# A planner's constants and one yield: new estimates for the order of a fused transformer trunk

## The chip, the cores and the metric

The kernel runs on one core of a Trainium2 chip. The metric is the device time of one execution in microseconds (us); lower is better. An execution is timed without the profiler several times, and once with it.

## What is computed

The reference is a trunk of two layers on 256 tokens of width 1024, all in float32. Each layer is, cut to what matters:

```python
h = h + 0.5 * swiglu(rmsnorm(h, ffn1_norm), ffn1_w_gate, ffn1_w_up, ffn1_w_down)   # 1024 -> 2752 -> 1024
u = rmsnorm(h, mix_norm)
z = u @ w_in                       # mLSTM q, k, v, o, i, f; attention q, k, v; two merge gates
hm = sigmoid(m_o) * head_rmsnorm(mlstm_chunkwise(mq, mk, mv, ig, lf))
ha = swa_gqa_sinks(aq, ak, av, a_sinks)          # 16 query heads, window 128
h = h + (sigmoid(g_m) * (hm @ w_branch_m) + sigmoid(g_a) * (ha @ w_branch_a)) @ w_out
h = h + 0.5 * swiglu(rmsnorm(h, ffn2_norm), ffn2_w_gate, ffn2_w_up, ffn2_w_down)
h = h + sigmoid(rmsnorm(h, ple_norm) @ ple_gate_w) * (p_i @ ple_proj_w)
```

## The kernel before

**Precision.** Every float32 operand of a matmul is split into a high and a low half of the type fp32r, `hi = cast(x)` on ScalarE and `lo = x - hi` on VectorE. A product is three matmuls: `xh·wh`, `xh·wl`, `xl·wh` (`mm3`). In the profile the halves of the weights are the tiles `wh` and `wl`, those of the normed activations `uT`.

**Tiles.** The 256 tokens are two token tiles (t = 0, 1) of 128 rows; the residual stream is `h0`, `h1`. A weight is loaded in pieces of one megabyte (`raw`, two buffers), each of two parts of 128x1024 values; a part is split into a ring of eight `wh`, `wl` buffers. A part of 128x1024 covers two blocks of 128 input features for 512 outputs.

**Stages.** In each layer: FFN 1, the mixer, FFN 2, and the gate on the layer's end (`ple`). An FFN starts with 512 gate and 512 up features by token (`gu`), goes on by feature (`pg`, `pu`) and ends with the down projection (`dn`). The mixer starts with attention's projections (`kvq`) and ends with the output projection (`yo`). `ple` first multiplies the per-layer input (`pp`, 24 matmuls) and then the gate (`pg`, 1024 outputs in two halves n = 0, 1). The tile `pg` is thus both FFN and layer-end gate.

**From one stage to the next.** At the end of a stage the two token tiles are finished one after the other. `sink` adds a half-row of 512 to `h` (VectorE), squares it with a sum (`sq`, ScalarE), and after the second half starts the next norm: `ms` (VectorE), a power of -1/2 on GpSimd (`r`), two scaled halves `xn` (VectorE), eight transposes `tp` on TensorE, and the split into `uT`. While that runs for token tile 0, TensorE has the rest of token tile 1: 22 matmuls after a `dn`, 24 after `yo`, 30 after the gate. For the gate, `use` puts ahead of the sum a tanh (ScalarE) and a product (VectorE), both on the tile `sg`.

**The order.** The four engines TensorE, ScalarE, VectorE and SyncE run their instructions in exactly the order in which the Python program writes them. What interleaves the stages is a planner that runs while the program is written. Side work is a generator (a chain); each `yield` marks a step. A class `Clock` keeps an estimated time for each engine: an instruction costs `fixed + n * per` (`COST`, for n values a row), a result counts for other engines `SYNC` later, and a load of a megabyte occupies the queue for `DMA[1]` and lands `DMA[0]` later. `now` is the estimated time of TensorE. Between groups of matmuls (every three of 512 columns in the stages named here) `tick` continues each chain whose last step is ready by that estimate, and then `feed` may begin the split of one more weight part, if its piece has landed by the estimate and ScalarE and VectorE are not too far ahead:

```python
    def tick(self):
        for chain in list(self.bg):
            if chain[1] <= self.clock.now:
                self.advance(chain)
        self.feed()
```

So the estimates change no instruction, but they decide where each one stands in its engine's order. `haste`, set near the end of token tile 0, holds further splits back once three parts are in store, until token tile 0's transposes are written. When a matmul needs a chain that isn't finished, `finish` moves the estimated clock forward until it is.

**The opening.** Row sets of `x` and the first pieces are loaded in the order: token tile 0 in two halves, first gate piece in two halves, token tile 1, second gate piece. The planner sets `ready` for the two norms from these loads.

## Time and profile before

| | |
|---|---|
| median of 3 runs | 1383.12 us (1381.99 to 1383.64) |
| profiled execution | 1383.27 us, span 1381.5 us, granted clock 0.998 |
| TensorE matmuls | 1366.2 us busy, 99% of the span, 9056 instructions |
| VectorE | 860.7 us, 62% |
| ScalarE | 734.8 us, 53% |
| GpSimd | 55.4 us, 4% |
| DMA | 243.81 MB, 176 GB/s on average |

In the rows of the profile that follow, the first number of a timeline row is the start in us from the begin of the span, the second the duration, then the engine, the operation, the tile written and those read, shapes, and in brackets the idle time of that engine before it and what ended it. PE is TensorE's matmuls, DVE is VectorE, ACT is ScalarE, POOL is GpSimd. Almost all rows carry the line L130, a helper that passes every instruction on, so the tile's name tells what a row is. In rows of busy time by stretch the columns are the stretch, its length, then busy time and count of PE, PEld, DVE, ACT and POOL, the granted clock of TensorE, the DMA share and GB/s.

### The profile page before, as it was taken

The numbers are of one execution on the slowest core, as the hardware profiler recorded it, in microseconds if no ns is written. First come the engines' busy times: TensorE is split into PE (matmuls) and PEld (weight loads), VectorE is DVE, ScalarE is ACT, GpSimd is POOL, SyncE is SP. The second block draws the span as 40 slices with busy tenths as digits, with TensorE's granted clock in tenths as the row PEclk, the third lists the DMA queues.
The fourth block names the chain that finished last, engine by engine and source line by source line (L and its number), as shares of the span: only waits on it lengthen the run. The fifth ranks groups of instructions, "written<-read, shape, count | busy, mean of one in ns | idle before, by whom it ended". The sixth has DMA issues, their size and how long they took to land.

```text
span 1381.5 us, 21941 instructions
## 1 busy us (share of the span) xinstructions
PE 1366.2 (99%) x9056; PEld 1233.3 (89%) x9056; DVE 860.7 (62%) x1213; ACT 734.8 (53%) x1146; POOL 55.4 (4%) x84
## 2 busy tenths in 40 slices
PE   8999999999999999999999999999999999999998
PEld 5999887899899899988879998878998998999886
DVE  5655458767786665554565554687677876554544
ACT  5554346878465444443454443477785554544433
POOL 0000012000000000000000000120000000000000
PEclk9999999999999999999999999999999999999999
DMA  6665636344645565565456566445456544755651
GB/s 206 222 212 168 229 125 212 123 138 110 226 153 185 167 213 186 169 232 184 158 162 213 170 199 213 152 154 173 106 143 206 181 156 164 220 190 187 209 180 61
DMA packets 125830, 243.81 MB, mean 176 GB/s; under 512 B 14977, under 2 KB 23841, under 8 KB 125730
## 3 DMA queue, kind: packets, MB, share of 16 engines
q1 hardware_dynamic: 125730, 242.41, 55.1%
q8 instruction: 71, 1.16, 0.4%
q14 instruction: 29, 0.24, 0.1%
HBM read 241.34 MB, written 1.05 MB: 175 GB/s over the span
## 4 chain that ended last, share of the span: by engine, by line
PE 96%; DMA 1%; DVE 1%; ACT 1%; issue 0%; POOL 0%; SPq 0%; ACTq 0%; POOLq 0%
PE dn L130 17%; PE pg L130 16%; PE pu L130 14%; PE gu L130 7%; PE z L130 7%; PE gt L130 7%; PE kvq L130 5%; PE ya L130 3%; PE v L130 3%; PE ym L130 3%; PE yo L130 3%; PE og L130 3%; PE tp L130 3%; PE sc L130 1%; PE ha L130 1%; DMA raw<-in_ffn_w_gate_dram 1%
## 5 line engine op out<-in xcount | busy, mean ns | idle before, releaser
L130 DVE TENSOR_TENSOR wl<-raw,wh 128x1024 fp32r<-128x1024 f32 (+1 forms) x448 | 540.2, 1222 | 351.3 <-ACT wh L130 348.5
L130 ACT CAST wh<-raw 128x1024 fp32r<-128x1024 f32 x448 | 460.5, 1050 | 414.1 <-PE dn L130 82.9
L130 PE MATMUL dn<-wh,hid 128*128 128x512 f32 x688 | 218.1, 395 | 0.0
L130 PE MATMUL pg<-uT,wh 128*128 128x256 f32 x1088 | 194.0, 281 | 0.0
L130 PE MATMUL pu<-uT,wh 128*128 128x256 f32 x1088 | 192.9, 280 | 0.0
L130 PEld LDWEIGHTS pg<-uT,wh 128*128 128x128 f32 x1088 | 166.4, 188 | 0.2
L130 PEld LDWEIGHTS pu<-uT,wh 128*128 128x128 f32 x1088 | 166.2, 188 | 0.0
L130 PEld LDWEIGHTS dn<-wh,hid 128*128 128x128 f32 x688 | 129.2, 188 | 30.2
L130 PE MATMUL pg<-uT,wl 128*128 128x256 f32 x544 | 152.4, 280 | 0.0
L130 PE MATMUL pu<-uT,wl 128*128 128x256 f32 x544 | 152.2, 280 | 0.0
L130 PE MATMUL dn<-wl,hid 128*128 128x512 f32 x352 | 139.0, 395 | 0.0
L130 PEld LDWEIGHTS pu<-uT,wl 128*128 128x128 f32 x544 | 102.4, 188 | 0.0
L130 PEld LDWEIGHTS pg<-uT,wl 128*128 128x128 f32 x544 | 102.3, 188 | 0.0
L130 PE MATMUL z<-uT,wh 128*128 128x256 f32 x512 | 93.5, 284 | 0.0
L130 PE MATMUL gt<-uT,wh 128*128 128x256 f32 x512 | 93.1, 283 | 0.0
L130 PE MATMUL gu<-wh,uT 128*128 128x512 f32 x256 | 83.4, 402 | 2.2 <-ACT uT L130 2.2
L130 PEld LDWEIGHTS gt<-uT,wh 128*128 128x128 f32 x512 | 78.8, 188 | 1.2
L130 PEld LDWEIGHTS dn<-wl,hid 128*128 128x128 f32 x352 | 66.1, 188 | 15.1
L130 PEld LDWEIGHTS z<-uT,wh 128*128 128x128 f32 x512 | 78.8, 188 | 0.6
L130 PE MATMUL z<-uT,wl 128*128 128x256 f32 x256 | 71.9, 281 | 0.0
L130 PE MATMUL gt<-uT,wl 128*128 128x256 f32 x256 | 71.8, 280 | 0.0
L130 PE MATMUL kvq<-wh,uT 128*128 128x512 f32 x192 | 63.7, 401 | 0.0
(194 smaller groups left out, 2037.7 us busy)
## 6 DMA issues: line engine op xcount, KB each, us to landing
raw<-in_w_in_dram SPq DMA_DIRECT2D x60, 1024.0 KB, 5.1
raw<-in_ffn_w_up_dram SPq DMA_DIRECT2D x40, 1024.0 KB, 5.1
raw<-in_ffn_w_down_dram SPq DMA_DIRECT2D x40, 1024.0 KB, 5.2
raw<-in_ffn_w_gate_dram SPq DMA_DIRECT2D x39, 1024.0 KB, 5.5
raw<-in_w_branch_a_dram SPq DMA_DIRECT2D x16, 512.0 KB, 5.9
raw<-in_w_branch_m_dram SPq DMA_DIRECT2D x8, 1024.0 KB, 5.1
raw<-in_w_out_dram SPq DMA_DIRECT2D x8, 1024.0 KB, 5.2
raw<-in_ple_gate_w_dram SPq DMA_DIRECT2D x8, 1024.0 KB, 8.0
```

Source lines behind the costliest of these rows:

```text
L130: return issue(*args, **kw)
```

## The change

The estimates get other values, an instruction with a sum along the row (`accum_out`) costs `SUM` more, and in `ple` the use of token tile 1's gate waits in the planner, in layer 0 alone, until token tile 0's `xn` of the next norm are written down. `normed` counts the norms of token tile 0 so far, four a layer.

```diff
-    COST = {"tensor": (0.0, 1 / 2400), "scalar": (0.12, 1 / 1120), "vector": (0.12, 1 / 960), "gpsimd": (0.3, 0.17)}
-    SYNC = 0.1
+    COST = {"tensor": (0.0, 1 / 2250), "scalar": (0.14, 1 / 1130), "vector": (0.16, 1 / 960), "gpsimd": (0.5, 0.17)}
+    SYNC = 0.2
+    SUM = 0.2
     TABLE = 1.4
-    DMA = (1.0, 2.9)
+    DMA = (2.0, 2.9)
...
-    def charge(self, engine, n, func=None):
+    def charge(self, engine, n, func=None, extra=0.0):
...
-        self.t[engine] = start + fixed + n * per
+        self.t[engine] = start + fixed + extra + n * per
...
                               args[2] if op == "activation" else None)
+                              self.clock.SUM if kw.get("accum_out") is not None else 0.0)
...
     def norm(self, t, ss, g, xT):
...
             nc.vector.scalar_tensor_tensor(xn[n], self.h[t][:, half(n)], r, g[n], op0=ALU.mult, op1=ALU.mult)
+        self.normed += t == 0
         yield
...
     def ple(self, l, xT, sink):
...
             def use(n, t, ps):
+                while t == NT - 1 and l < DEPTH - 1 and self.normed <= 4 * (l + 1):
+                    yield
                 sg = self.scr("sg")
                 nc.scalar.activation(sg, ps, AF.Tanh, scale=0.5)
```

## The prediction

> **What bounds the kernel now.** I read the totals of the page first, then the waits of TensorE, then the timeline engine by engine where those waits lie.

> ```profile
> span 1381.5 us, 21941 instructions
> PE 1366.2 (99%) x9056; PEld 1233.3 (89%) x9056; DVE 860.7 (62%) x1213; ACT 734.8 (53%) x1146; POOL 55.4 (4%) x84
> ```

> TensorE is busy for 1366.2 of 1381.5 us. No matmul is added or removed, so an order can only fill the 15.3 us that are left, or add to them. The waits of TensorE, in total, times and longest:

> ```profile
> PE tp L130 <- DVE xn L130: 3.9, 2, 3.0
> PE gu L130 <- ACT uT L130: 2.2, 1, 2.2
> PE sc L130 <- DVE ptd L130: 0.9, 2, 0.5
> PE gu L130 <- DVE wl L130: 0.8, 1, 0.8
> ```

> The 3.0 is the boundary between the layers. The 2.2, the 0.8 and 0.9 of the 3.9 lie in the opening, and the 0.9 in attention. Everything else follows without a gap.

> **The boundary between the layers.** Rows of TensorE, ScalarE, VectorE and GpSimd there:

> ```profile
> 690.55 0.40 PE L130 MATMUL pg<-wh,uT 128*128 128x512 f32 x1
> 693.93 1.88 PE L130 MATMUL tp<-ident,xn 128*128 128x128 f32 x8 [2.98 <-DVE xn L130]
> 697.86 0.40 PE L130 MATMUL gu<-wh,uT 128*128 128x512 f32 x1
> 698.09 0.39 PE L130 MATMUL gu<-wl,uT 128*128 128x512 f32 x1
> 702.41 0.50 PE L130 MATMUL gu<-wl,uT 128*128 128x512 f32 x1
> 686.88 1.05 ACT L130 CAST wh<-raw 128x1024 fp32r<-128x1024 f32 x1 [1.20 <-DMA raw<-in_ffn_w_gate_dram]
> 687.84 0.59 ACT L130 ACTIVATE sg<-pg 128x512 f32<-128x512 f32 x1
> 693.25 0.63 ACT L130 ACTIVATE sq<-h 128x512 f32<-128x512 f32 x1 [1.48 <-DVE h L130]
> 696.33 1.99 ACT L130 CAST wh<-raw 128x1024 fp32r<-128x1024 f32 x2
> 698.22 0.60 ACT L130 ACTIVATE sg<-pg 128x512 f32<-128x512 f32 x1
> 691.79 0.69 DVE L130 SCALAR_TENSOR_TENSOR sg<-sg,pp 128x512 f32<-128x512 f32 x1 [0.32 <-ACT sg L130]
> 693.13 1.41 DVE L130 SCALAR_TENSOR_TENSOR xn<-h,r,g 128x512 f32<-128x512 f32 x2
> 701.14 2.35 DVE L130 TENSOR_TENSOR wl<-raw,wh 128x1024 fp32r<-128x1024 f32 x2
> 691.55 0.55 POOL L130 TENSOR_TENSOR r<-ms,mhalf 128x1 f32<-128x1 f32 x1 [23.93 <-DVE ms L130]
> 693.90:697.80 3.90, 3.87 (x14) 3.41 (x15) 2.02 (x3) 2.61 (x5) 0.00 (x0) 0.56 0.02 4
> ```

> A matmul of 512 columns follows the last after 0.23 us (697.86 to 698.09). The 24 matmuls of token tile 1 ahead of 690.55 put the end of tile 0's gate at about 685.2. Its tanh runs only at 687.84, because a weight cast that waits for its DMA stands ahead on ScalarE. POOL has the norm's factor at 692.10, but xn starts at 693.13: the pair sg, h of tile 1's first half (691.79 to 693.2) stands ahead on VectorE. TensorE idles 2.98 us. Then the clock is at 0.56 of full speed (last row) until 697.8, and transposes and six matmuls take 3.93 us where 0.8 + 6 x 0.23 = 2.2 would do. The place costs about 3.0 + 1.7 = 4.7 us.

> **The change there.** The new condition makes tile 1's use (tanh, sg, h, square) wait in the planner until tile 0's xn are written down. VectorE then has xn at 692.14 in place of 693.13, 1.0 us sooner. How many matmuls the planner puts ahead of the transposes I work out by its own constants: tanh, two products, mean, power come to 2.77 us before and 3.41 after, which is 13.0 and 15.0 matmuls of its length (512/2400, 512/2250); it looks every 3 matmuls, so both resume at 15; xn end at 21.6 and 22.0, so both place the transposes after 24 of 30. The six matmuls stay behind them.

> Queued behind the moved work: on VectorE sg and h (2 x 0.7) now follow xn, which ends at 692.14 + 1.41 = 693.55, so h ends at 694.9; the square behind it on ScalarE needs 0.75, and the casts uT stand behind the square: they start at about 695.6, where they now start at 695.0. After them come two weight casts (1.99), tile 1's tanh, its two products, square and mean, and only then the wl at 701.14, which takes 2.92 us from that tanh. TensorE uses the first of these wl after 18 matmuls of gu: 697.86 + 4.2 = 702.03, and gets it at 702.41. So **the next thing that is late is wl**, and it does not come sooner: 696.33 becomes about 696.6, wl ends 0.2 to 0.3 later. TensorE starts gu a microsecond sooner and waits at the fourth gate part. Against that, a later DMA estimate (from 3.9 to 4.9 us for a megabyte) may move the weight cast's VectorE half behind the mean, 0.3 sooner. I take 0 for this place. Ends: +0.3 (as worked out), and -1.1 if the cast of 686.88 goes behind the tanh altogether: the chain then starts 2.3 us sooner, the square of tile 1 ends at 694.1, wl at 701.3.

> **The other boundaries.** Here the costs alone act, as the new condition holds at once. From FFN to mixer, rows of TensorE, ScalarE and VectorE:

> ```profile
> 197.49 1.03 PE L130 MATMUL tp<-ident,xn 128*128 128x128 f32 x8
> 198.28 0.48 PE L130 MATMUL dn<-wh,hid 128*128 128x512 f32 x1
> 198.59 0.39 PE L130 MATMUL dn<-wl,hid 128*128 128x512 f32 x1
> 198.85 0.48 PE L130 MATMUL kvq<-wh,uT 128*128 128x512 f32 x1
> 198.12 1.08 ACT L130 CAST uT<-tp 128x512 fp32r<-128x512 f32 x2
> 198.74 1.29 DVE L130 TENSOR_TENSOR uT<-tp,uT 128x512 fp32r<-128x512 f32 x2 [1.28 <-ACT uT L130]
> ```

> After tile 0's last sum there are 22 matmuls of tile 1. Old reckoning: h 0.75, square 0.68, mean 0.22, power 0.57 = 2.22 us, resumed at matmul 11 (2.35); xn 1.31 + 0.1 ends at 3.75 = 17.6 matmuls; next look at 20. The rows agree: two dn follow the transposes. New: h 0.89, square 0.79 + 0.2 (with its sum and the longer SYNC), mean 0.36, power 0.87 = 3.12 us = 13.7 matmuls, resumed at 14 (3.19); xn 1.39 + 0.2 ends at 4.77 = 20.97; next look at 22. So the two dn go ahead and nothing is left to cover uT. From the start of the transposes to the first uT takes 198.12 + 0.59 - 197.49 = 1.22 us, to the first low half 198.74 + 0.69 - 197.49 = 1.94. With transposes at 198.0 the third kvq matmul, which needs the low half, runs at 199.95 in place of 199.49; allowing for the matmul's own delay there, 0.38 us lost. It occurs in both layers: **+0.8**.

> From mixer to FFN:

> ```profile
> 477.38 1.03 PE L130 MATMUL tp<-ident,xn 128*128 128x128 f32 x8
> 478.17 0.47 PE L130 MATMUL yo<-wh,mT 128*128 128x512 f32 x1
> 478.94 0.40 PE L130 MATMUL gu<-wh,uT 128*128 128x512 f32 x1
> ```

> 24 matmuls are left, looked at every 3. Old: resumed at 12 (2.56), xn end at 3.97 = 18.6, placed at 21; three yo follow the transposes (478.17 to 478.94), as reckoned. New: resumed at 15 (3.41), xn end at 5.00 = 21.97, placed at 24, behind all yo. Transposes then start at 478.07, the low half is there at 480.0, where the third matmul of gu ran at 479.41: 0.56 us. Two layers: **+1.1**. From FFN to the gate of the layer's end the transposes slip as well, but 24 pp matmuls (5.6 us) lie ahead of the first use: 0.

> **The opening.** Rows of ScalarE, VectorE and TensorE:

> ```profile
> 8.29 1.04 ACT L130 CAST wh<-raw 128x1024 fp32r<-128x1024 f32 x1 [2.96 <-DMA raw<-in_ffn_w_gate_dram]
> 9.62 1.04 ACT L130 CAST wh<-raw 128x1024 fp32r<-128x1024 f32 x1 [0.29 <-DMA raw<-in_ffn_w_gate_dram]
> 10.57 1.07 ACT L130 CAST uT<-tp 128x512 fp32r<-128x512 f32 x2
> 11.53 0.64 ACT L130 ACTIVATE sq<-h 128x512 f32<-128x512 f32 x1
> 13.51 2.00 ACT L130 CAST wh<-raw 128x1024 fp32r<-128x1024 f32 x2 [0.64 <-DMA raw<-in_ffn_w_gate_dram]
> 14.34 1.41 DVE L130 SCALAR_TENSOR_TENSOR xn<-h,r,g 128x512 f32<-128x512 f32 x2 [0.67 <-POOL r L130]
> 15.67 1.22 DVE L130 TENSOR_TENSOR wl<-raw,wh 128x1024 fp32r<-128x1024 f32 x1
> 11.21 0.79 PE L130 MATMUL gu<-wh,uT 128*128 128x512 f32 x1 [2.24 <-ACT uT L130]
> 16.94 0.50 PE L130 MATMUL gu<-wl,uT 128*128 128x512 f32 x1 [0.80 <-DVE wl L130]
> ```

> Old reckoning: tile 0's xn are ready at 7.60, tile 1's rows at 8.50, so uT goes ahead of tile 1's squares: the rows show it (10.57, 11.53). New: tile 0's rows at 5.15, squares to 6.94, mean to 7.30, power to 8.17, xn to 9.75; tile 1's rows at 9.50. Its two squares (1.27 us: 10.57 + 1.07 against 12.8) are now put ahead of uT, and both wl of the first pieces ahead of uT's low half. The squares need tile 1's rows. These are half a megabyte, in the queue behind the piece that landed at 9.62 and ahead of the megabyte that landed at 13.51; an equal rate gives 9.62 + 3.89/3 = 10.9 (an estimate from these rows). So uT starts at 12.2, gu at 12.9 in place of 11.21: 1.7 later. Part comes back: wl at 15.67 now goes ahead of tile 1's xn and ends at 15.8, so the 0.80 is gone. But tile 1's transposes fall behind all 18 matmuls and uncover 0.4. The matmuls are slow at first, as a row of the busy times by stretch shows:

> ```profile
> 11.20:14.70 3.50, 3.50 (x8) 2.76 (x9) 2.83 (x5) 2.86 (x7) 0.55 (x1) 1.00 0.12 44
> ```

> Eight matmuls in 3.5 us are 0.44 each, nearly twice 0.23 (though the clock column says 1.00 there). With 3.5 us of that again from 12.9, the twenty-first matmul runs at 20.7 in place of 19.5: **+1.2**. Ends: +0.4 (rows landing by 9.6) and +2.0. The high end is a matter of when the slow stretch ends. If it ends on a grid of its own length, and not that long after the restart, the end after 14.7 is 18.2; from 12.9 the matmuls run at 0.44 until then, the twenty-first at 21.4, and the opening loses 1.9. [...]

> **Sum.** +1.2 + 0.8 + 1.1 + 0 = +3.1 us. The profiled execution took 1383.27 us, 0.15 over the median 1383.12; on the median this is 1386.2. Attention and recurrence change order too: their chains grow by about a tenth in matmuls, and TensorE's 0.9 us there can go or grow to 2: ends -0.9, +2.

> **Rivals.**
> - *The transposes stay.* The new places miss the old ones by one matmul in each case (20.97 against a look at 20, 21.97 against 21). If VectorE or ScalarE work is reckoned otherwise by that much, the 1.9 us vanish: 1384.3. Against it: the old reckoning met all four places exactly. Chance 0.17.
> - *Not slower: the boundary between the layers is cured.* If the DMA estimate moves the cast of 686.88 behind the tanh and wl ahead of tile 1's second half, all 4.7 come back: 1386.2 - 4.7 = 1381.5. It decides from 1 us: the cast's megabyte is issued early enough in the planner's time that I find its place 1.0 us ahead of the tanh under the new latency (2.4 before). Chance 0.17; with the opening unharmed as well it would pass below 1380.4.
> - *The busy window.* The slow stretch ends on its grid: the opening loses 1.9, 1386.9; and a recurrence chain late at ym adds up to 2: 1389. Chance 0.18.

> The forecast itself has 0.48 (own range 1385.3 to 1387.2). About 0.2% (2.8 us) is what a measurement of this kernel can tell from no change. Slower by more, above 1385.9: 0.30 of the 0.48 and most of the window's 0.18, together 0.46. Faster: half of the cure's 0.17 and a little, 0.10. Same: 0.44. The range, to leave no more than 2 in 10 out: 1381.5 to 1388.5.

> **What would show it.** Transposes of xn directly ahead of kvq and gu, with waits of TensorE on uT that aren't there now; squares ahead of uT in the opening and gu near 12.9; xn ahead of sg at the boundary between the layers, and gu waiting for wl at about 702 there. Wrong if the first gu comes before 11.5, if gu at that boundary runs through its fourth gate part before 701, or if the dn and yo rows after the transposes remain.

## The result and the profile after

The changed kernel takes 1402.37 us in the median (1401.27 to 1403.76, 4 runs) against 1382.55 us of the kernel before on the same chip: a ratio of 1.0151, 95% interval [1.0138, 1.0163]. It is slower by about 20 us, where 3 had been forecast. The profiled execution took 1403.76 us.

The totals of the changed kernel and its waits of TensorE (what was waited for, total us, times, longest; two waits ahead of the opening's `gu` and one of 0.5 on `mT` are left out):

```profile
span 1402.0 us, 21877 instructions
PE 1376.5 (98%) x9056; PEld 1238.5 (88%) x9056; DVE 858.0 (61%) x1213; ACT 734.9 (52%) x1148; POOL 52.6 (4%) x84
PE gu L132 <- ACT uT L132: 6.7, 5, 2.9
PE sc L132 <- ACT pr L132: 3.1, 3, 1.1
PE kvq L132 <- DVE wl L132: 1.8, 1, 1.8
PE kvq L132 <- ACT uT L132: 1.6, 2, 1.4
PE ym L132 <- DVE hmT L132: 1.1, 1, 1.1
PE ym L132 <- ACT hmT L132: 1.0, 1, 1.0
PE gu L132 <- DVE wl L132: 0.9, 2, 0.5
```

Two things grew. Waits stand where there were none (`sc` on `pr`, `kvq`, `ym`), and the busy time of the same 9056 matmuls is 10.3 us longer (1376.5 against 1366.2), half of the loss, which no wait accounts for. A halved clock, shown below, makes by estimate about 3.4 of it (three stretches of 1.7 us against one before) and a longer slow stretch in the opening about 1 (six more matmuls at 0.43 us in place of 0.23); the rest is spread over the stages and was not assigned. Both kernels run the same weight matmuls in the same sequence, so the start of the first matmul of a stage can be compared one to one:

| stretch | later by (us) | of which seen as |
|---|---|---|
| start to `dn`, layer 0 | +1.80 | first `gu` at 12.25 in place of 11.21, fourteen slow matmuls in place of eight |
| `dn`, `kvq` of layer 0 | +1.92 | wait of 1.36 on `uT` |
| attention and recurrence, layer 0 | -0.10 | a wait of 1.02 made good |
| `ym`, layer 0 | +5.90 | waits 0.99 and 1.13 on `hmT`, halved clock |
| `yo`, `gu`, layer 0 | +1.66 | wait of 1.20 on `uT` |
| FFN 2 | -0.17 | |
| gate of layer 0 to the features of layer 1 | -2.45 | the place that the condition is meant for |
| `dn`, `kvq`, layer 1 | +4.29 | wait of 1.78 on `wl`, halved clock |
| attention and recurrence, layer 1 | +2.55 | waits 1.06, 1.02 on `pr`, halved clock |
| `ym`, `yo`, `gu`, layer 1 | +4.56 | wait of 1.20 on `uT`, one on `mT` |
| the rest | +0.6 | |

The sum is +20.6. The boundary for which the prediction gave 0 is the only place that gained more than 0.2. The following rows are all of the changed kernel.

FFN to mixer, layer 0; timeline rows of TensorE, ScalarE and VectorE:

```profile
199.82 1.04 PE L132 MATMUL tp<-ident,xn 128*128 128x128 f32 x8
202.21 0.50 PE L132 MATMUL kvq<-wh,uT 128*128 128x512 f32 x1 [1.36 <-ACT uT L132]
200.97 0.63 ACT L132 ACTIVATE sq<-h 128x512 f32<-128x512 f32 x1 [2.12 <-DVE h L132]
201.60 1.05 ACT L132 CAST uT<-tp 128x512 fp32r<-128x512 f32 x2
200.25 0.68 DVE L132 SCALAR_TENSOR_TENSOR h<-dn,h 128x512 f32<-128x512 f32 x1
```

The transposes stand behind all `dn`, as forecast. But between them and their casts ScalarE has token tile 1's square, which waits for token tile 1's `h`, which needs the last `dn`. The cast starts at 201.60, 1.78 us after the first transpose, where the kernel before took 0.63 us (197.49 to 198.12): by that measure 1.1 us late.

The recurrence's end, `ym` of layer 0; the same engines:

```profile
453.68 0.38 PE L132 MATMUL ym<-hmT,wh 128*128 128x256 f32 x1 [0.99 <-ACT hmT L132]
455.19 0.54 PE L132 MATMUL ym<-hmT,wh 128*128 128x256 f32 x1 [1.13 <-DVE hmT L132]
451.36 2.00 ACT L132 CAST wh<-raw 128x1024 fp32r<-128x1024 f32 x2
453.25 0.38 ACT L132 CAST hmT<-tp 128x256 fp32r<-128x256 f32 x1
452.44 2.36 DVE L132 TENSOR_TENSOR wl<-raw,wh 128x1024 fp32r<-128x1024 f32 x2 [0.53 <-ACT wh L132]
454.72 0.42 DVE L132 TENSOR_TENSOR hmT<-tp,hmT 128x256 fp32r<-128x256 f32 x1
```

For token tile 1 both halves of the last head's `hmT` stand behind two weight casts each, 2.00 us on ScalarE and then 2.36 us on VectorE.

Mixer's start in layer 1, VectorE and TensorE:

```profile
898.11 1.03 PE L132 MATMUL tp<-ident,xn 128*128 128x128 f32 x8
901.85 0.51 PE L132 MATMUL kvq<-wl,uT 128*128 128x512 f32 x1 [1.78 <-DVE wl L132]
899.37 1.29 DVE L132 TENSOR_TENSOR uT<-tp,uT 128x512 fp32r<-128x512 f32 x2 [1.90 <-ACT uT L132]
900.57 3.49 DVE L132 TENSOR_TENSOR wl<-raw,wh 128x1024 fp32r<-128x1024 f32 x3
```

Three `wl` whose `wh` is long there stand behind token tile 1's `uT`. VectorE idles 1.90 us for that `uT`, and then TensorE idles 1.78 us for the first of the three.

The clock, in rows of busy time by stretch:

```profile
199.27:202.68 3.41, 2.05 (x14) 1.49 (x12) 1.71 (x6) 1.71 (x5) 0.55 (x1) 1.00 0.00 0
451.86:455.27 3.41, 1.28 (x10) 0.85 (x8) 2.75 (x4) 1.76 (x3) 0.00 (x0) 1.00 0.79 303
455.27:458.68 3.41, 3.41 (x16) 3.41 (x17) 0.00 (x0) 1.05 (x1) 0.00 (x0) 0.50 0.75 244
899.00:902.41 3.41, 1.63 (x8) 1.04 (x7) 3.04 (x4) 0.82 (x2) 0.00 (x0) 1.00 0.00 0
902.41:905.82 3.41, 3.41 (x9) 2.63 (x8) 2.25 (x5) 0.00 (x0) 1.01 (x1) 0.50 0.83 266
936.54:939.95 3.41, 1.55 (x7) 0.80 (x6) 1.98 (x5) 3.40 (x17) 3.41 (x2) 1.00 0.00 0
939.95:943.36 3.41, 3.19 (x16) 2.26 (x16) 1.86 (x7) 2.92 (x11) 0.41 (x9) 0.50 0.00 0
```

After the stretches with 2.13, 1.78 and 1.86 us without a matmul (3.41 less the PE column) the clock is at 0.50 for 3.41 us, which costs by estimate up to half of that, 1.7 us. After 1.36 us without a matmul (first row) it stays at 1.00, until 455.27. So the wait of 1.78 us at `kvq` cost by estimate up to 3.5 with what followed.

The opening (one row of it from the kernel before, line L130) and attention:

```profile
12.25 0.80 PE L132 MATMUL gu<-wh,uT 128*128 128x512 f32 x1 [2.88 <-ACT uT L132]
17.96 0.58 PE L132 MATMUL gu<-wl,uT 128*128 128x512 f32 x1
18.38 0.63 PE L132 MATMUL gu<-wh,uT 128*128 128x512 f32 x2
18.85 0.40 PE L132 MATMUL gu<-wl,uT 128*128 128x512 f32 x1
14.78 0.65 PE L130 MATMUL gu<-wh,uT 128*128 128x512 f32 x2
10.39 0.63 ACT L132 ACTIVATE sq<-h 128x512 f32<-128x512 f32 x1 [0.20 <-DMA h<-in_x_dram]
11.63 1.05 ACT L132 CAST uT<-tp 128x512 fp32r<-128x512 f32 x2
245.58 0.38 PE L132 MATMUL sc<-band,identb 128*128 128x512 bf16 x1 [1.02 <-ACT pr L132]
241.33 1.28 ACT L132 ACT_TABLE_LOAD   x1
```

In the opening both squares of token tile 1 are ahead of `uT`, as forecast; its rows landed by 10.39, half a microsecond sooner than estimated. The matmuls are slow for longer than before: fourteen of them, one every 0.43 us, from 12.25 until 18.38, where the spacing falls to 0.23 (two in 0.47 us). In the kernel before, eight were slow, from 11.21 until 14.78. In attention the next scores wait 1.02 us for eight exponentials (242.63 to 245.44) that stand behind the table load of 1.28 us.

The boundary between the layers:

```profile
696.33 0.60 ACT L132 ACTIVATE sg<-pg 128x512 f32<-128x512 f32 x1 [0.30 <-PE pg L132]
705.07 1.05 ACT L132 CAST uT<-tp 128x512 fp32r<-128x512 f32 x2
705.68 0.50 PE L132 MATMUL gu<-wh,uT 128*128 128x512 f32 x1 [1.19 <-ACT uT L132]
711.15 0.50 PE L132 MATMUL gu<-wl,uT 128*128 128x512 f32 x1 [0.51 <-DVE wl L132]
```

ScalarE idles 0.30 us until token tile 0's gate is done and then runs its tanh at once; no cast with a DMA wait stands ahead of it any more. But the transposes stand behind 27 of token tile 1's 30 matmuls and not 24, and `uT` is 1.19 us late behind a square of token tile 1. `wl` is late at the fourth gate part, as forecast, by 0.51.

### The profile page after: what moved, and what is told of

It is laid out like the page before. It is cut to its first block, busy times and chain, and to the rows that moved or that the text cites. A ratio compares the mean times of both kernels' runs of the same rounds, so it can differ in the third digit from the quotient of the medians.

```text
span 1402.0 us, 21877 instructions
## 1 busy us (share of the span) xinstructions
PE 1376.5 (98%) x9056; PEld 1238.5 (88%) x9056; DVE 858.0 (61%) x1213; ACT 734.9 (52%) x1148; POOL 52.6 (4%) x84
## 3 DMA queue, kind: packets, MB, share of 16 engines
HBM read 241.34 MB, written 1.05 MB: 173 GB/s over the span
## 4 chain that ended last, share of the span: by engine, by line
PE 93%; DVE 3%; ACT 2%; DMA 1%; issue 1%; SPq 0%; POOL 0%; ACTq 0%
PE dn L132 17%; PE pg L132 15%; PE pu L132 14%; PE gu L132 7%; PE z L132 7%; PE gt L132 7%; PE kvq L132 5%; PE ya L132 3%; PE og L132 3%; PE yo L132 3%; PE v L132 3%; PE ym L132 3%; PE tp L132 2%; PE sc L132 1%; PE ha L132 1%; DVE wl L132 1%
## 5 line engine op out<-in xcount | busy, mean ns | idle before, releaser
L132 PEld LDWEIGHTS gu<-wh,uT 128*128 128x128 f32 x256 | 49.1, 193 | 21.2 <-ACT uT L132 8.2
```

The lines of the kernel that those rows point to most:

```text
L132: return issue(*args, **kw)
```

## Experiments

**The condition alone.** All constants as before (and SUM 0); only this stays of the change:

```diff
+        self.normed += t == 0
...
+                while t == NT - 1 and l < DEPTH - 1 and self.normed <= 4 * (l + 1):
+                    yield
```

> The old constants with the new condition alone. Up to the boundary between the layers its order is that of before, so what it changes lies there. Theory Y (the 2.8 us that the changed kernel wins at that boundary come from the condition): 1379.5 to 1381.5. Rival C (they come from the constants, which move a weight cast behind the tanh; the condition alone only brings the next wait forward, as the prediction had it): 1382.3 to 1383.3.

1381.63 us, ratio 1.0001 [0.9992, 1.0010]. TensorE's waits at the boundary, from its timeline:

```profile
691.63 1.32 PE L132 MATMUL tp<-ident,xn 128*128 128x128 f32 x8 [1.30 <-DVE xn L132]
694.86 0.50 PE L132 MATMUL gu<-wh,uT 128*128 128x512 f32 x1 [0.52 <-ACT uT L132]
701.28 0.50 PE L132 MATMUL gu<-wl,uT 128*128 128x512 f32 x1 [1.49 <-DVE wl L132]
```

The 2.98 us on `xn` become 1.30, and 0.52 on `uT` and 1.49 at `wl` come back, the latter on the matmul that the prediction named. The time lies between the two ranges expected; the condition alone is worth nothing that can be measured.

**The constants alone,** without the condition:

```diff
-                while t == NT - 1 and l < DEPTH - 1 and self.normed <= 4 * (l + 1):
-                    yield
```

> All new constants without the condition. Both theories have the loss of 23 us at the other places here. Theory Y: 1404.5 to 1406 (the boundary's 2.8 us gone). Rival C: 1401.5 to 1403, as with the condition.

1399.12 us, 1.0128 [1.0110, 1.0146], below both ranges expected. The loss is the constants'. Its runs lie between 1396.07 us at a mean granted clock of 1.0 and 1402.39 at 0.996: the same program, by the mean clock with and without halved stretches (an estimate: the profile is of the first). From the gate of layer 0 to the end of layer 1's first `gu` it gains 4.1 us, where the changed kernel gains 2.8: with these constants the condition costs 1.3 there.

**One constant at a time,** on the kernel before, without the condition. First the DMA latency:

```diff
-    DMA = (1.0, 2.9)
+    DMA = (2.0, 2.9)
```

> Of the change only the later landing of a load, DMA 1.0 to 2.0. Theory S (slower estimates of the steps and of SYNC make the loss: transposes and recurrence come too late): little, 1382 to 1386. Rival L (the later landing makes it: weight splits come in bunches and stand ahead of the chains): 1392 to 1399.

1391.08 us, 1.0069 [1.0055, 1.0083], between the two ranges. Then all but the DMA latency:

```diff
-    DMA = (2.0, 2.9)
+    DMA = (1.0, 2.9)
```

> Of the change only COST, SYNC and SUM; landing as before, no condition. Theory S: most of the loss, 1396 to 1404. Rival L: 1385 to 1390. If both parts add up, the excess of this one and of the one with the landing alone make some 23 us.

1401.02 us, 1.0145 [1.0130, 1.0161]. By the medians the two parts cost 9.9 and 19.8 us, and 17.9 together: they don't add. TensorE's waits on `wl` in the latter:

```profile
PE gu L132 <- DVE wl L132: 3.9, 3, 1.8
PE kvq L132 <- DVE wl L132: 3.5, 2, 1.8
```

Four of them are the wait of 1.76 us behind token tile 1's transposes, in both layers at `kvq` and at the `gu` that follows the mixer. Behind those that end at 493.30 and 902.58 the matmuls run 0.43 us apart for a while, behind the one that ends at 210.66 they run 0.23 apart. Here the transposes stand behind the last `dn` and `yo` too, without token tile 1's square in between, and the two places of layer 0 lose 0.43 and 0.41 us.

TensorE's cost per column alone:

```diff
-    COST = {"tensor": (0.0, 1 / 2400), "scalar": (0.12, 1 / 1120), "vector": (0.12, 1 / 960), "gpsimd": (0.3, 0.17)}
+    COST = {"tensor": (0.0, 1 / 2250), "scalar": (0.12, 1 / 1120), "vector": (0.12, 1 / 960), "gpsimd": (0.3, 0.17)}
```

> Of the change only TensorE's estimate, 1/2400 to 1/2250; transposes then keep their places at the stage boundaries. Theory E (a slower TensorE in the reckoning lets attention's scores come sooner, counted in matmuls, than their PSUM banks are free; the other costs make the boundaries and the recurrence late): score waits on ScalarE's pr of about 1 us each in attention, no loss at the boundaries or at ym, 1382 to 1385. Rival (all the loss hangs on the longer chains alone): no new waits, 1380.5 to 1381.5.

1387.38 us, 1.0041 [1.0027, 1.0055], above both ranges. No wait on `pr` came up; 2.28 us on `qn` in layer 1 did. And the latency between engines alone:

```diff
-    SYNC = 0.1
+    SYNC = 0.2
```

> Of the change only SYNC, 0.1 to 0.2. Theory E: transposes behind the last matmul at every boundary, 0.4 to 0.6 us lost at each of the four, recurrence late at ym, no score waits on pr: 1387 to 1398. Rival (the fixed costs and SUM make the loss, SYNC little): 1381 to 1384.

1410.68 us, 1.0212 [1.0196, 1.0228], above both ranges and more than the whole change, with the four waits of 1.76 again and a row of its own in each layer, here of layer 0:

```profile
290.26 1.04 PE L132 MATMUL tp<-ident,pr 128*128 128x128 f32 x4 [2.19 <-DVE qT L132]
```

**SYNC put back.** If SYNC were the harmful one, taking it back in the changed kernel should help:

```diff
-    SYNC = 0.2
+    SYNC = 0.1
```

> The changed kernel with SYNC back at 0.1; everything else is new. Alone, SYNC 0.2 costs 29 us, the other constants less. Theory S (SYNC is what puts the casts and sums in harmful places, because it is added at each step of each chain): the transposes remain behind all dn and yo matmuls (0.4 to 0.5 us each, four places), one wl more goes ahead of tile 1's uT at kvq in the order, and the time is 1386 to 1392. Theory J (any constant that moves a look by one step costs this much; the sum of the others keeps the loss): 1396 to 1403.

1401.79 us, 1.0141 [1.0125, 1.0156]: theory S falls. The wait at `kvq` goes, and seven waits on `wl` at `gu` (9.9 us) come. Neither SYNC nor the DMA latency is needed for the loss: without either one it is 1401.79 and 1401.02 us. The fixed costs of the other engines and `SUM` were not tried one by one. Each set of constants tried put the waits in other places.

**Three orders put right.** These edits change no constant; they name what stands ahead of what. In the changed kernel, first, token tile 1's last half-row waits in the planner until token tile 0's `uT` casts are written (`moved`):

```diff
...
         def then(n, t, y):
+            while following is not None and (n, t) == (1, NT - 1) and not moved:
+                yield
```

> The changed kernel, with one thing more: at the end of every stage the sum, square and mean of tile 1's second half wait in the planner until tile 0's transposes and uT casts are written down. Theory F (the waits of 1.2 to 1.4 us at the stage boundaries come from tile 1's square standing ahead of the uT casts on ScalarE): these waits fall to 0.2 to 0.5 us and the kernel to 1397 to 1400.5. Rival (they come from the later transposes alone): waits stay over 1 us, 1401.5 to 1403.

1401.13 us, 1.0143 [1.0128, 1.0158], between the two ranges. Three waits on `uT` (1.36, 1.20, 1.20) fell to 0.24 each, the one between the layers stayed at 1.19, and layer 0's `dn` to `kvq` lost 0.44 in place of 1.56. But a wait of 1.75 on `wl` came up at `kvq` of layer 0, beside the one that layer 1 had already (1.78, now 1.76), and the waits on `wl` at `gu` rose from 0.9 to 2.2 us, so little was left of it. Second, the low halves of weight parts go ahead of token tile 1's `uT`; tried first with the kernel that has four such waits (all but the DMA latency, no condition; `splits` lists the parts begun):

```diff
...
         yield
+        if t == NT - 1:
+            for chain in self.splits:
+                self.advance(chain)
         for n in range(2):
             self.to_T(xn[n], xT, n * 4, t)
```

> The kernel with the new engine costs, SYNC and SUM alone (1401.0 us, +19.5), and one more edit: before token tile 1's transposes of a norm are written down, the low halves of all weight parts whose high half is written down are written down too, so that on VectorE they stand ahead of uT's low half and not behind it. Theory W (the wait of 1.76 us at kvq and gu is an order on VectorE, three wl behind a uT whose transposes TensorE has just run, and such a wait then halves the clock for 3.4 us, 1.7 us each): the four waits on wl after tile 1's transposes vanish (4 x 1.76 = 7.0) and with them the clock drops that followed (one to three, 1.7 each), so 1389 to 1393 us. Rival B (VectorE and ScalarE have too much work there in whatever order): uT's low half, now behind three wl, is late in their place, and the time stays at 1398 to 1402.

1391.82 us, 1.0078 [1.0064, 1.0091], about 9 us less. VectorE at `kvq` of layer 1:

```profile
893.56 4.63 DVE L132 TENSOR_TENSOR wl<-raw,wh 128x1024 fp32r<-128x1024 f32 x4
898.11 1.28 DVE L132 TENSOR_TENSOR uT<-tp,uT 128x512 fp32r<-128x512 f32 x2
```

Four `wl`, then `uT`, with no idle time between, and no wait on `wl` longer than 0.15 us is left in that kernel. VectorE had the time there; the order wasted it. Both edits in the changed kernel:

> The changed kernel with two edits of order: tile 1's second-half sum and square wait until tile 0's uT casts are written down (alone: 1401.1), and the low halves of weight parts stand ahead of tile 1's uT. Theory W: the four waits on uT of 1.2 to 1.4 us fall to 0.25 (4.4 us) and the waits on wl behind tile 1's transposes (1.78 in the profile of the changed kernel, more in the other) are gone as well, with one or two of the three clock drops: 1402.4 - 4.4 - 1.8 - 1.7 to 3.4 = 1393 to 1395. Attention and recurrence keep their losses. Rival B (no slack in the order, each cure moves the wait): 1399 to 1403.

1395.58 us, 1.0104 [1.0089, 1.0118], half a microsecond above theory W. What is left is mainly `ym`: +5.7 and +5.3 us, with waits of 0.99 and 1.13 in both layers and, by the mean clock of 0.997, halved stretches. Third, then, the last head's casts are written directly behind its transposes:

```diff
         for t in range(NT):
-            yield from tr.transposing(self.og[t][:, hd * MD : (hd + 1) * MD], self.hmT, 2 * hd, t, 2)
+            src = self.og[t][:, hd * MD : (hd + 1) * MD]
+            if hd == MH - 1:
+                tr.to_T(src, self.hmT, 2 * hd, t, 2)
+            else:
+                yield from tr.transposing(src, self.hmT, 2 * hd, t, 2)
```

> The changed kernel with the two edits of order that brought it to 1395.6 us, and a third: the last head's transposes into hmT write their high and low casts down at once, so that these stand ahead of the weight parts' casts on ScalarE and VectorE. Theory H (ym loses 5.5 us in each layer through two waits on hmT of 0.99 and 1.13 us, and through the halved clock that follows when both fall into one 3.4 us window, 1.7 us): both waits fall under 0.4, no low-clock stretch follows ym, and the time is 1387.5 to 1389.5. Rival M (the loss at ym is that the last head's num products now lie in ym's stretch and end late in whatever order): the wait moves to wl or to the last head's scale, 1392 to 1396.

1387.05 us, 1.0043 [1.0026, 1.0059]. ScalarE in `ym` of layer 0:

```profile
448.25 0.65 ACT L132 CAST hmT<-tp 128x256 fp32r<-128x256 f32 x2 [2.27 <-PE tp L132]
448.78 2.01 ACT L132 CAST wh<-raw 128x1024 fp32r<-128x1024 f32 x2
```

No wait on `hmT` is left, and the mean clock is 1.0 where it was 0.997. The later place of the last head as such costs the 1.2 to 1.8 us that `ym` still loses, of which `gt` had given 0.9 to 1.0.

**The boundary alone.** Can the gain be had without the loss? With old constants, the condition, splits held back until token tile 0's `ms` is written, and three more looks of delay for token tile 1's second half:

```diff
+                if t == NT - 1 and n == 1 and l < DEPTH - 1:
+                    for _ in range(3):
+                        yield
...
-        if not must and self.haste and self.store >= HASTE:
+        if not must and (self.hold or self.haste and self.store >= HASTE):
```

> The old constants, the new condition, and two things at the boundary between the layers alone: no weight split is begun from the last two parts of tile 0's gate until its tanh to mean are written down, and the second half of tile 1 waits three looks more, so that the wl of the next gate parts stand ahead of its products. If the prediction's account of that place holds (the cast ahead of the tanh costs 2.3 us, wl is late next), the place gains 3 to 4.5 us: 1377 to 1378.5. Rival (something else is late next there): 1379.5 to 1381.5.

1381.47 us, 0.9999 [0.9991, 1.0008]: the tanh came in time, but 1.17 us on `uT` and 0.99 on `wl` took the place. At last the new constants from token tile 1's last `dn` of layer 0's FFN 2 to the end of layer 1's first `gu`, the old ones elsewhere, no condition:

```diff
+                        if self.downs == 2 and (t, n, k) == (1, 0, late):
+                            self.clock.estimate(True)
...
             self.project(units, xT, "gu", use, first=first)
+            if self.downs == 2:
+                self.clock.estimate(False)
```

> The kernel before with the new constants in force only between tile 1's last down products of layer 0's second FFN and the end of layer 1's first gate and up products, without the new condition; everywhere else the old constants. The order there is the one of the kernel with all constants and no condition, in which tile 0's tanh no longer stands behind the cast that waits for its DMA, and the boundary gained 4.1 us of its profile. Theory L (what the new constants gain is that place alone, and what they lose is elsewhere): 1377 to 1378.5 us. Rival: the gain in the profile was mostly the clock drop of 694 us, which most executions of the kernel before do not have: 1379 to 1380.5. Rival N: no change, since the next thing is late as with the condition alone: 1381 to 1382.

1379.20 us (11 runs) against 1380.86 (15 runs), 0.9986 [0.9977, 0.9995]: 0.14% or 1.9 us faster than the kernel before, a small difference that the interval still holds clear of 1. That is in the first rival's range, not in theory L's. ScalarE and TensorE there:

```profile
684.65 0.60 ACT L139 ACTIVATE sg<-pg 128x512 f32<-128x512 f32 x1 [0.78 <-PE pg L139]
698.04 0.50 PE L139 MATMUL gu<-wl,uT 128*128 128x512 f32 x1 [0.81 <-DVE wl L139]
```

The tanh is in time, TensorE waits there for neither `xn` nor `uT`, and `wl` is still next, by 0.81. Profile against profile the place gained 4.0 us by the same measure, the medians differ by 1.7. The likely rest is the halved stretch that the shown profile of the kernel before has at 694 us: its executions in this comparison lie between 1380.07 and 1383.17 us at clocks from 1.0 to 0.998, so many seem to run without it.

## Why the prediction was wrong, step by step

**The places held, their prices did not.** The transposes behind all `dn`, all `yo`, after 18 matmuls in the opening, and the squares ahead of `uT` came as worked out. So did the price of the slip alone: 0.38 and 0.56 forecast, 0.43 and 0.41 measured where token tile 1's square does not come between, 0.44 with token tile 1's last half held back. But in the changed kernel these boundaries of layer 0 lost 1.56 and 1.38 us up to the next stage's first matmul. The step that failed here is "resumed at 14": it took VectorE for free. By the planner's own account VectorE had 0.19 us of other work left at that moment, so the norm went on at matmul 17 and not 14, its `xn` were ready only after the next stage's first look, and at that look token tile 1's `h` and square were written first. From mixer to FFN it was the same: 0.41 us left, resumed at 18 and not 15. The edit that reverses that order alone removed the wait (1.36 to 0.24).

**The opening** was forecast at +1.2 from a first `gu` at 12.9. It came at 12.25, because the rows landed sooner, but the slow matmuls behind it lasted 6.1 us and not 3.5. The two errors work against each other, so that the loss of 1.80 lies within the ends of 0.4 to 2.0 is in part luck.

**The boundary between the layers** was forecast at 0 and gave -2.45. The low end, "the cast of 686.88 goes behind the tanh altogether", is what happened, but its price of -1.1 left out that the halved clock goes with the wait, and that `wl` is then only 0.51 late. With the condition alone, without that, the reasoning held to the matmul: `wl` is next, gain nothing.

**Attention and recurrence** were bounded at +2 in all. `ym` alone took 5.90 in layer 0. By the table, attention, recurrence and `ym` make 9.8 of the 20.6 us (-0.10, 5.90, 2.55 and, in layer 1, 1.49 at `ym`): this is the term most mis-sized. The bound came from the waits that the trace before shows there, 0.9 us together; it did not ask what stands on ScalarE and VectorE directly ahead of `hmT` when the last head comes later. One order of casts, the third of the three edits, was worth 8 us over both layers where both lost by it.

**Weight parts** had no term at the mixer's start. `wl` behind token tile 1's `uT` cost 1.78 us and a halved stretch in layer 1.

**The clock** had a term at two places where the trace before shows it. In the changed kernel the one at 694 us is gone, and three others cost by estimate up to 5.1 us, 1.7 each.

Of the rivals, "the transposes stay" did not occur. "The boundary is cured" was half right (2.45 of its 4.7) and decided nothing. "The busy window", by which the slow stretch ends on a grid, came nearest. No run had shown such a grid when it was forecast; in the two profiles of the last section the ends of the slow stretches lie on one. In the opening it had the slow matmuls until 18.2 and a loss of 1.9, measured 18.38 and 1.80, and it named a chain late at `ym`, but at up to 2 us where the two layers lost 5.90 and 1.49. The sign was right, for reasons that explain some 4 of the 20 us: the opening's 1.8 and four slips of 0.4 to 0.6; for the rest it was luck. The three edits of order take 1.0151 to 1.0043, some 15 us of the 20; the other 6 (the opening, the slips of 0.4 to 0.8, the later last head, less the gain between the layers) were not separated further.

## What to carry to other kernels

Where a planner's estimates only set an order, closer estimates are not a better order (of TensorE, for one: 512 columns take 0.23 us, where the old constant has 0.213 and the new one 0.228): each constant tried moved the waits at several places at once, the parts did not add, and the best version used the new values in one place only. So price such a change by what will stand directly ahead of each late-needed cast on its engine (`uT`, `hmT`, `wl`), not by how far a chain slips; here the slips cost 0.4 us each, the casts behind a megabyte's split 1 to 2 (0.99 to 1.78). And price a wait of TensorE together with the clock behind it: the wait of 1.78 us at `kvq` was followed by 3.41 us at 0.50, by estimate up to 1.7 us more.

## What the runs showed of the hardware

Cut along these steps from 20 us up to the last matmul, the two profiles have four stretches with 1.78 us or more without a matmul: 690.66 in the kernel before (2.98 us) and 451.86, 899.00 and 936.54 in the changed one (2.13, 1.78 and 1.86). Each was followed by a halved one. No other has more than 1.36, and none of the others was followed by a halved one. In the kernel with all but the DMA latency and the low halves first, 2.55 us (699.35 to 702.76) were followed by 3.41 us at 0.50; with SYNC alone, 1.72 us (904.79 to 908.20) by 3.41 us at 1.00. The kernel with token tile 0's `uT` casts first has 1.76 us in this first row, and 1.00 in the next:

```profile
901.30:904.71 3.41, 1.65 (x8) 1.05 (x7) 3.37 (x4) 0.50 (x2) 0.00 (x0) 1.00 0.00 0
904.71:908.12 3.41, 3.41 (x17) 2.78 (x16) 2.25 (x5) 0.00 (x0) 1.01 (x1) 1.00 0.94 323
```

The length of the waits alone does not tell which are followed by a slow stretch: of the waits of 1.76 us in the kernel with all but the DMA latency, the two that end at 493.30 and 902.58 were, and the one that ends at 210.66 was not. The kernel with the constants alone has the two waits on `hmT` too (0.99 and 1.14, `ym` of layer 0, ending at 452.24 and 453.76), here cut between them:

```profile
449.04:452.45 3.41, 2.42 (x20) 2.15 (x19) 1.87 (x3) 2.54 (x4) 0.00 (x0) 1.00 0.67 203
452.45:455.86 3.41, 2.27 (x18) 2.11 (x18) 1.25 (x2) 1.05 (x1) 0.00 (x0) 1.00 0.59 184
455.86:459.27 3.41, 3.41 (x31) 3.41 (x30) 3.14 (x5) 1.76 (x3) 0.00 (x0) 1.00 0.62 233
```

The clock stays at 1.00, and 31 matmuls run in the third where the changed kernel ran 16. That can explain how runs of one program spread over 6 us: those of this kernel lie 6.3 us apart at mean clocks of 1.0 and 0.996, and 0.004 of 1400 us is 5.6 us, an estimate.
